# A hybrid encoder trunk: another order of the block steps, the norm and the table load where its stages meet

## The chip, the cores and the metric

The kernel runs on one core of a Trainium2 chip. The metric is the device time of one execution in microseconds. TensorE does the matrix products, VectorE (DVE), ScalarE (ACT) and GpSimd (POOL) the rest, and SyncE issues the loads of the weights.

## The reference

512 tokens and 16 learned meta tokens (528 in all) of width 1024, float32, pass two layers, each of three residual sub-layers behind an RMS norm:

```
for i in range(DEPTH):                                   # 2
    h = h + 0.5 * swiglu(rmsnorm(h, ffn1_norm[i]), ffn1_w_in[i], ffn1_w_out[i])
    hn = rmsnorm(h, mix_norm[i])
    h = h + (diff_attention(hn, ...) if i % 2 == 0 else gla_mixer(hn, ...))
    h = h + 0.5 * swiglu(rmsnorm(h, ffn2_norm[i]), ffn2_w_in[i], ffn2_w_out[i])
return rmsnorm(h, final_norm)[:, N_META:]
```

swiglu(h) is (silu(h @ w_g) * (h @ w_u)) @ w_out with an inner width of 2816. The attention is a differential one over 8 heads, block-causal; GLA is gated linear attention over 4 heads in chunks of 64.

## The kernel before, in words

**Stages.** The program is written out as a fixed order of instructions, and each engine runs its own in that order. The stages are a (SwiGLU), attention ("da"), b, c (SwiGLU of the next layer), GLA, and d. The residual stream lies in SBUF with features on partitions, as eight blocks `xr[0..7]` of 128 features by 528 tokens.

**Products.** A float32 operand is split into a high part (rounded, made by ScalarE) and a low part (the difference, made by VectorE); a product is three matrix products, high by high, high by low and low by high. Weights are split the same way as they come.

**A SwiGLU stage** (`ffn`, L679). The inner width is 22 blocks. A plain block takes four units S1, S3, S2, S4 of 24 matrix products. The others take seven units P1 to P7 of 12 products each, by a scheme with sums of quarters of the operands (`in_units`, L560). S1 and S3 read even blocks of the stream, S2 and S4 odd ones. The class `in_stream` (L568) lists the weight tasks: "cut" (ScalarE L637 makes the high part, VectorE L662 the low part) and "add" (VectorE L651, sums of weight quarters, four per block of seven). Split weights lie in a ring of nine slots. `to(n)` (L673) cuts the first n; in the stage, after each unit, tasks are issued until the weights lead by `AHEAD` = 6 units (L916 to L920). The second product of the stage (`out_piece`, L844, matrix products L857) works in six slabs of inner blocks; the last slab is the tail (L939 to L956).

**The norm** is not applied to the input but to the result of the first product, as a scale per token. `add_square` (L334) squares a finished block on ScalarE (L340) and adds it up on POOL (L344). `rms_scale` (L377) loads a function table into ScalarE (L370), sums over partitions by two matrix products with ones (L384), and makes the scale R by logarithm, exponential and a Newton step (L349 to L356). It is called behind unit S3 of block 0, in stage a behind S4 of block 1 (L929). A unit's result is scaled as it leaves PSUM (L734); where R does not exist yet it is copied (L736) and scaled later (L717). The units of plain blocks use four PSUM banks, so P1, the first unit of the next block, needs the bank of S1 and S2 to be empty.

**The end of a stage.** When block j of the output is done, VectorE adds it to the stream (L873 in a SwiGLU stage, L541 behind attention and GLA). Then `follow` (L502) starts the block's way into the next stage, a generator `next_block` (L462). For kind "seven" (into b, c, d) its steps are: on ScalarE the plain split's high part (L420), the square, and the scaled form (L434); on VectorE the low part (L425, two halves of an even block, one piece of an odd one) together with sums of quarters (L444 for an even block, L446 to L448 for an odd one); for an odd block then ScalarE's high part of the sums (L454); and VectorE's low part (L456). For kind "parts" (into attention and GLA) they are ScalarE's L468 and square, and VectorE's L471. `follow` first takes one step of every pending generator (`go_on`), then the new block's first step, then one more step of the old ones. So the steps of block j-1 come behind the addition of block j. `drain` takes what is left.

Behind attention and GLA, `finish_all` (L294) ends blocks 0 to 2 and collects what follows; blocks 3 to 7 run one after another (L1461), and at the start of each, `take` (L237) may split a chunk of the projection's weights two blocks ahead (ScalarE L223, VectorE L226). `ahead` is the next stage's weight stream: it is started behind block 5 and cut to 2, to 4 behind block 6 and to 5 at the end. In b's tail the same stands in `nxt.to(j - 2)` behind block j from 3 on. Output pairs of PSUM banks alternate between two places, so a block's products wait for the addition of the block before last.

Of the kernel before, what the change touches and what calls it, by code (L numbers as in the profile page):

```python
# [104 lines left out]
def hybrid_trunk_kernel(  # L105
# [271 lines left out]
    def rms_scale(acc, name, c0=0):  # L377
        hn = (L - c0) // 2
        table(LN_EXP)
# [82 lines left out]
    def next_block(kind, gcol, acc, j, c0, z=None):  # L462
# [11 lines left out]
        elif kind == "seven":  # L474
# [6 lines left out]
            rest()  # L481
            sums(i, tok, z[i], k)
# [11 lines left out]

    def go_on():
        for x in list(pending):
            try:
                next(x)
            except StopIteration:
                pending.remove(x)  # L500

    def follow(gen=None):  # L502

        go_on()
        before = list(pending)
        if gen is not None:
            next(gen, None)
            pending.append(gen)
        for x in before:
            try:  # L510
                next(x)
            except StopIteration:
                pending.remove(x)
# [19 lines left out]
    def project_out(nk, rhs, coef, gnext, name, tokens_only, c_next, apart=None):  # L533
# [4 lines left out]
        def out_block(j):  # L538
            def done(ps):
                for pv, xv in evacuation(ps, xr[j], tokens_only, j == apart):  # L540
                    dve.scalar_tensor_tensor(xv, pv, coef, xv, op0=ALU.mult, op1=ALU.add)  # L541
                rest = lambda: follow(next_block("seven", gnext, acc, j, c_next, z))
                if patient[0]:
                    later.append(rest)
# [134 lines left out]
    def ffn(stream, gain, acc, name, gnext, kind, nxt, aside=(), head=None, tok=False, behind=None):  # L679
# [8 lines left out]
        with tc.tile_pool(name=f"h_{name}", bufs=1) as hp:  # L688
# [22 lines left out]
            late = []  # L711
            bare = []
# [157 lines left out]
            def out_done(s, j):  # L870
                ps = outs.pop((s, j))
                for pv, xv in evacuation(ps, xr[j], tok):
# [29 lines left out]
            for i, u in enumerate(work):  # L902
# [4 lines left out]
                else:  # L907
                    product(*u)
                if behind and i <= KD:
# [9 lines left out]
                for _ in range(-(-(goal - stream.done) // between)):  # L919
                    stream.step()  # L920
# [3 lines left out]
                if len(u) == 3:  # L924
                    if u[2] == pieces(u[0]) - 1:
                        out_done(*u[:2])
                else:
                    evacuate(*u)
                    if u == ((1, "S4") if head else (0, "S3")):  # L929
                        R.append(rms_scale(acc, name, c0))  # L930
                        scale_bare()
                    if aside and u[1] in ("P4", "S4"):
# [6 lines left out]
            for j in range(KD):  # L939
# [7 lines left out]
                if j == 1 and kind == "parts":  # L947
# [3 lines left out]
                    load_to(2)  # L951
                out_done(tail, j)
                if kind == "parts" and j in (5, 6):
                    split_to(j - 5)
                if kind == "seven" and j >= 3:
                    nxt.to(j - 2)  # L956
# [95 lines left out]
    def diff_attention(acc, gnext, ahead):  # L1052
# [6 lines left out]
        with ExitStack() as es:  # L1059
# [401 lines left out]
            for j, b in enumerate(blocks[3:], 3):  # L1461
                run(b)
                if j == 5:
                    ahead.start()
                    ahead.to(2)
                if j == 6:
                    ahead.to(4)
            drain()
            ahead.to(5)
# [34 lines left out]
    def gla(acc, gnext, ahead):  # L1504
# [5 lines left out]
        with ExitStack() as es:  # L1510
# [346 lines left out]
            for j, b in enumerate(blocks[3:], 3):  # L1857
                run(b)
                if j == 5:
                    ahead.start()  # L1860
                    ahead.to(2)
# [161 lines left out]
```

## Time and profile before

| what | value |
|---|---|
| runs shown | 2094.09, 2098.22, 2100.36 us; median 2098.22 |
| the profiled execution | 2095.57 us |
| its span, first to last instruction | 2093.8 us |
| mean granted TensorE clock | 0.981 |
| matrix products | 14672 |
| VectorE, ScalarE, POOL instructions | 3095, 2046, 193 |

In rows of a timeline the first two numbers are the start and the length in microseconds from the start of the span, and the bracket at the end is the idle time of the engine ahead of the row with what ended it; xN is the number of instructions merged into the row. A row of the waits names who waited for whom, then the total, the times and the longest.

### The profile page before, as it was taken

Reading aid. Unit: us, or ns where it says so; the run is one execution under the profiler, and the core shown is the slowest. Engines: PE = TensorE matmul, PEld = TensorE weight load, DVE = VectorE, ACT = ScalarE, POOL = GpSimd, SP = SyncE. Lnnn points to the kernel's source line nnn. Section 1 sums busy time; section 2 is a strip of 40 time slices with the busy share of each in tenths; the row PEclk is TensorE's granted clock in tenths of the full one; section 3 lists DMA queues with packets and bytes.
Section 4 is the critical chain, followed back from the end, with each engine's and each line's share of the span. In section 5 each row is a group of like instructions: output and inputs, shape, how many; then the busy total and the mean of one; then the engine's idle time right before and its main releaser. Section 6 shows DMA issues by size and latency. Waiting matters only on the chain.

```text
span 2093.8 us, 36697 instructions
## 1 busy us (share of the span) xinstructions
PE 1984.3 (95%) x14672; PEld 1875.5 (90%) x14672; DVE 1681.0 (80%) x3095; ACT 1023.1 (49%) x2046; POOL 263.6 (13%) x193
## 2 busy tenths in 40 slices
PE   7899999999899989999997999999899989999997
PEld 7899999877787979999997999999788878999995
DVE  7888887688888789888878988887666678988884
ACT  6444444455555554444445444444654555544443
POOL 2000000534332200000001000000633210000002
PEclk9999999999999999999999999999999999999998
DMA  4233323111111223333322333332122222333331
GB/s 146 88 103 107 96 97 107 51 51 41 41 42 40 71 81 109 99 101 99 104 77 67 111 101 97 98 102 85 55 78 73 64 91 82 116 100 98 106 101 41
DMA packets 66285, 178.73 MB, mean 85 GB/s; under 512 B 7345, under 2 KB 13618, under 8 KB 66114
## 3 DMA queue, kind: packets, MB, share of 16 engines
q1 hardware_dynamic: 65792, 176.25, 27.1%
q8 instruction: 115, 1.88, 0.4%
q14 instruction: 56, 0.46, 0.1%
q10 hardware_dynamic: 322, 0.13, 0.0%
HBM read 174.26 MB, written 2.10 MB: 84 GB/s over the span
## 4 chain that ended last, share of the span: by engine, by line
PE 72%; DVE 18%; ACT 6%; issue 3%; POOL 0%; DMA 0%; SPq 0%; DVEq 0%; ACTq 0%; POOLq 0%
PE ps_ao L857 6%; PE ps_co L857 6%; PE ps_bA L806 6%; PE ps_bo L857 5%; PE ps_cA L806 5%; PE ps_aA L806 5%; PE ps_do L857 5%; PE ps_dA L806 4%; PE ps_bD L806 3%; PE ps_cD L806 3%; PE ps_aD L806 3%; PE ps_dak L270 2%; PE ps_dD L806 2%; DVE ra L662 2%; PE ps_bB L806 1%
## 5 line engine op out<-in xcount | busy, mean ns | idle before, releaser
L637 ACT CAST ra<-fa 128x512 fp32r<-128x512 f32 x630 | 376.2, 618 | 166.7 <-DVE fa L651 165.9
L662 DVE TENSOR_TENSOR ra<-fa,ra 128x512 fp32r<-128x512 f32 x630 | 425.5, 685 | 22.2 <-ACT ra L637 16.4
L651 DVE TENSOR_TENSOR fa<-fa 128x512 f32<-128x512 f32 x328 | 219.7, 686 | 2.8
L834 DVE TENSOR_TENSOR ra<-fa,ra 128x512 fp32r<-128x512 f32 (+1 forms) x160 | 101.4, 636 | 68.0 <-ACT ra L833 66.7
L226 POOL TENSOR_TENSOR ra<-fa,ra 128x1024 fp32r<-128x1024 f32 x51 | 123.7, 2427 | 154.2 <-ACT ra L223 130.3
L806 PE MATMUL ps_bA<-ra 128*128 128x264 f32 x1008 | 134.7, 286 | 5.0 <-DVE ftb L734 4.0
L806 PE MATMUL ps_cA<-ra 128*128 128x264 f32 x1008 | 134.1, 285 | 4.8 <-DVE ftc L734 3.6
L806 PE MATMUL ps_dA<-ra 128*128 128x256 f32 x1008 | 132.1, 283 | 5.0 <-DVE ftd L734 3.1
L806 PEld LDWEIGHTS ps_dA<-ra 128*128 128x128 f32 x1008 | 127.8, 190 | 9.5 <-issue 3.3
L806 PEld LDWEIGHTS ps_bA<-ra 128*128 128x128 f32 x1008 | 127.8, 190 | 5.9 <-issue 4.2
L806 PEld LDWEIGHTS ps_cA<-ra 128*128 128x128 f32 x1008 | 127.2, 189 | 5.7 <-issue 3.7
L806 PE MATMUL ps_aA<-ra 128*128 128x264 f32 x912 | 122.1, 286 | 7.3 <-DVE fta L734 6.9
L806 PEld LDWEIGHTS ps_aA<-ra 128*128 128x128 f32 x912 | 115.8, 190 | 8.0 <-issue 7.1
L833 ACT CAST ra<-fa 128x512 fp32r<-128x512 f32 (+1 forms) x160 | 91.6, 575 | 0.0
L857 PE MATMUL ps_bo<-ra 128*128 128x264 f32 x624 | 86.0, 284 | 2.7 <-DVE xr L873 1.8
L857 PE MATMUL ps_co<-ra 128*128 128x264 f32 x624 | 85.8, 284 | 0.8 <-ACT ra L833 0.7
L857 PE MATMUL ps_ao<-ra 128*128 128x264 f32 x624 | 85.7, 283 | 0.9 <-DVE ra L834 0.9
L857 PE MATMUL ps_do<-ra 128*128 128x512 f32 x309 | 82.1, 395 | 0.9 <-ACT ra L833 0.7
L857 PEld LDWEIGHTS ps_bo<-ra 128*128 128x128 f32 x624 | 79.7, 188 | 3.5 <-issue 2.2
L857 PEld LDWEIGHTS ps_co<-ra 128*128 128x128 f32 x624 | 79.7, 188 | 1.3 <-ACT ra L833 0.9
L857 PEld LDWEIGHTS ps_ao<-ra 128*128 128x128 f32 x624 | 79.7, 188 | 1.1 <-DVE ra L834 1.1
L223 ACT CAST ra<-fa 128x1024 fp32r<-128x1024 f32 x64 | 66.8, 1046 | 4.3 <-issue 1.8
(529 smaller groups left out, 4341.7 us busy)
## 6 DMA issues: line engine op xcount, KB each, us to landing
fa<-in_f_in SPq DMA_DIRECT2D x174, 512.0 KB, 3.6
fa<-in_f_out SPq DMA_DIRECT2D x160, 256.0 KB, 2.7
fa<-in_da_in SPq DMA_DIRECT2D x24, 512.0 KB, 3.6
fa<-in_gla_in SPq DMA_DIRECT2D x24, 512.0 KB, 3.6
fa<-in_f_out SPq DMA_DIRECT2D x32, 128.0 KB, 2.1
fa<-in_da_out SPq DMA_DIRECT2D x8, 512.0 KB, 3.6
fa<-in_gla_out SPq DMA_DIRECT2D x8, 512.0 KB, 3.4
xr<-in_xT SPq DMA_DIRECT2D x8, 264.0 KB, 5.4
```

The lines of the kernel that those rows point to most:

```text
L223: act.copy(h, w)
L226: eng.tensor_tensor(out=l, in0=w, in1=h.bitcast(F32), op=ALU.subtract)
L270: nc.tensor.matmul(put(b, at, at + c1 - c0), w[:, ws], x[:, c0:c1], start=first, stop=last,)
L637: act.copy(self.parts(n)[0], self.source(i))
L651: dve.tensor_tensor(out=self.raw(f, x), in0=self.raw(f, a), in1=self.raw(f, b), op=ALU.add)
L662: dve.tensor_tensor(out=l, in0=self.source(i), in1=h.bitcast(F32), op=ALU.subtract)
L806: nc.tensor.matmul(banks[k, f], w[:, ws], v, start=(p in ("P1", "P2", "P7") and i == 0 and c == 0), stop=(i == NQ - 1 and c == 2), skip_gr ...
L833: act.copy(h, raw)
L834: dve.tensor_tensor(out=l, in0=raw, in1=h.bitcast(F32), op=ALU.subtract)
L857: nc.tensor.matmul(ps[:, b, : a1 - a0], w[:, ws], x[:, a0:a1], start=(f == f0 and i == 0), stop=(f == f1 - 1 and i == 2),)
```

## The change

It makes these edits. (1) In `next_block`, kind "seven", the low part and the sums become two steps. (2) `go_on` takes one step of the newest pending generator, one of each older one, then two more of the newest; it is called ahead of the addition of a block (behind it for blocks 0 to 2 of attention and GLA), and `follow` only takes the new block's first step. (3) The table load leaves `rms_scale`; it is issued behind block 3 of the tails of a, b and c, and in stage a ahead of its norm. (4) The norm is asked for behind unit S1 of block 0, in stage a behind S1 of block 2; a unit's evacuation while there is no R is issued behind the next unit's products. (5) In the first 16 items of a stage at most three weight tasks follow one item. (6) In b's tail `nxt.to(j - 2)` moves ahead of the addition of block j; behind attention and GLA the next stream is cut to 2 behind block 6 and to 3 at the end. (7) Stage a has four plain blocks instead of three and starts its ring two slots on; the two asides (lambda terms, gate weights) follow P4 units only.

```diff
     def rms_scale(acc, name, c0=0):
         hn = (L - c0) // 2
-        table(LN_EXP)
...
             yield
             rest()
+            yield
             sums(i, tok, z[i], k)
...
+    def steps_of(gen, n=1):
+        for _ in range(n):
+            try:
+                next(gen)
+            except StopIteration:
+                pending.remove(gen)
+                return
+
     def go_on():
-        for x in list(pending):
-            try:
-                next(x)
-            except StopIteration:
-                pending.remove(x)
-
-    def follow(gen=None):
-
-        go_on()
-        before = list(pending)
-        if gen is not None:
-            next(gen, None)
-            pending.append(gen)
+        if not pending:
+            return
+        *before, last = pending
+        steps_of(last)
         for x in before:
-            try:
-                next(x)
-            except StopIteration:
-                pending.remove(x)
+            steps_of(x)
+        if last in pending:
+            steps_of(last, 2)
+
+    def follow(gen):
+        next(gen, None)
+        pending.append(gen)
...
             def done(ps):
+                if not patient[0]:
+                    go_on()
...
                 if patient[0]:
-                    later.append(rest)
+                    later.append(lambda: (go_on(), rest()))
...
             def out_done(s, j):
                 ps = outs.pop((s, j))
+                if s == len(slabs) - 1:
+                    go_on()
...
                     product(*u)
+                    if waiting:
+                        evacuate(*waiting.pop())
+                    if u == ((2, "S1") if head else (0, "S1")):
+                        if head:
+                            table(LN_EXP)
+                        R.append(rms_scale(acc, name, c0))
+                        scale_bare()
...
-                for _ in range(-(-(goal - stream.done) // between)):
+                n_ = -(-(goal - stream.done) // between)
+                for _ in range(min(n_, 3) if i < 2 * KD else n_):
                     stream.step()
...
+                elif not R:
+                    waiting.append(u)
                 else:
                     evacuate(*u)
-                    if u == ((1, "S4") if head else (0, "S3")):
-                        R.append(rms_scale(acc, name, c0))
-                        scale_bare()
-                    if aside and u[1] in ("P4", "S4"):
+                    if aside and u[1] == "P4":
                         aside.pop(0)()
...
+                if kind == "seven" and j >= 3:
+                    nxt.to(j - 2)
                 out_done(tail, j)
+                if kind and j == 3:
+                    table(LN_EXP)
                 if kind == "parts" and j in (5, 6):
                     split_to(j - 5)
-                if kind == "seven" and j >= 3:
-                    nxt.to(j - 2)
...
                 if j == 5:
                     ahead.start()
+                if j == 6:
                     ahead.to(2)
-                if j == 6:
-                    ahead.to(4)
             drain()
-            ahead.to(5)
+            ahead.to(3)
...
-        "a": in_stream(f1_in[0], f1_out[0], 0, 3),
+        "a": in_stream(f1_in[0], f1_out[0], 2, 4),
```

## Rows read from the trace of the kernel before

**Rows 1.** The page's table of engines: busy us (share of the span) xinstructions.
```profile
PE 1984.3 (95%) x14672; PEld 1875.5 (90%) x14672; DVE 1681.0 (80%) x3095; ACT 1023.1 (49%) x2046; POOL 263.6 (13%) x193
```
**Rows 2.** The waits of TensorE over the whole span.
```profile
PE ps_dS L792 <- DVE ra L425: 4.5, 1, 4.5
...
PE ps_ss_gla L384 <- POOL acc_c L344: 3.1, 1, 3.1
```
**Rows 3.** The timeline of TensorE at the entries into a, b and c.
```profile
42.31 11.94 PE L792 MATMUL ps_aS<-ra 128*128 128x264 f32 x96
61.13 2.98 PE L806 MATMUL ps_aA<-ra 128*128 128x264 f32 x12 [6.88 <-DVE fta L734]
...
738.63 6.37 PE L792 MATMUL ps_bS<-ra 128*128 128x264 f32 x38 [4.52 <-DVE ra L425]
...
755.71 2.98 PE L806 MATMUL ps_bA<-ra 128*128 128x264 f32 x12 [3.97 <-DVE ftb L734]
...
1113.25 6.77 PE L792 MATMUL ps_cS<-ra 128*128 128x264 f32 x38 [5.57 <-DVE ra L425]
...
1130.33 2.36 PE L806 MATMUL ps_cA<-ra 128*128 128x264 f32 x12 [3.56 <-DVE ftc L734]
```
**Rows 4.** The timeline of VectorE from b's tail into c.
```profile
1088.56 0.71 DVE L873 SCALAR_TENSOR_TENSOR xr<-ps_bo,xr 128x528 f32<-128x528 f32 x1 [1.04 <-PE ps_bo L857]
...
1096.42 0.70 DVE L873 SCALAR_TENSOR_TENSOR xr<-ps_bo,xr 128x528 f32<-128x528 f32 x1
...
1098.40 0.42 DVE L448 SCALAR_TENSOR_TENSOR ftb<-ftb 128x264 f32<-128x264 f32 x1
1100.75 0.69 DVE L662 TENSOR_TENSOR ra<-fa,ra 128x512 fp32r<-128x512 f32 x1 [1.93 <-ACT ra L637]
1101.36 0.70 DVE L873 SCALAR_TENSOR_TENSOR xr<-ps_bo,xr 128x528 f32<-128x528 f32 x1
1101.97 1.25 DVE L456 TENSOR_TENSOR ra<-ftb,ra 128x1056 fp32r<-128x1056 f32 x1
1103.14 1.99 DVE L425 SCALAR_TENSOR_TENSOR ra<-xr,vec,ra 128x264 fp32r<-128x264 f32 x2
...
1110.93 0.70 DVE L873 SCALAR_TENSOR_TENSOR xr<-ps_bo,xr 128x528 f32<-128x528 f32 x1
...
1120.25 2.02 DVE L651 TENSOR_TENSOR fa<-fa 128x512 f32<-128x512 f32 x3
...
1125.27 0.43 DVE L350 TENSOR_SCALAR nA_c<-ps_ss_c 128x264 f32<-128x264 f32 x1 [0.96 <-ACT R_c L349]
...
1129.16 0.69 DVE L662 TENSOR_TENSOR ra<-fa,ra 128x512 fp32r<-128x512 f32 x1
```
**Rows 5.** The timeline of ScalarE behind attention (first row) and in b's tail.
```profile
716.73 1.04 ACT L223 CAST ra<-fa 128x1024 fp32r<-128x1024 f32 x1
...
1097.15 0.93 ACT L420 ACTIVATE ra<-xr,vec 128x264 fp32r<-128x264 f32 x2 [2.46 <-DVE xr L873]
...
1099.14 1.06 ACT L454 CAST ra<-ftb 128x1056 fp32r<-128x1056 f32 x1
1100.10 0.61 ACT L637 CAST ra<-fa 128x512 fp32r<-128x512 f32 x1
1102.09 0.74 ACT L420 ACTIVATE ra<-xr,vec 128x528 fp32r<-128x528 f32 x1 [1.38 <-DVE xr L873]
...
1103.90 0.60 ACT L637 CAST ra<-fa 128x512 fp32r<-128x512 f32 x1
...
1123.46 1.28 ACT L370 ACT_TABLE_LOAD   x1
```
**Rows 6.** The timeline of VectorE behind attention: additions 3 and 7, a chunk's split.
```profile
713.84 0.69 DVE L541 SCALAR_TENSOR_TENSOR xr<-ps_dao,xr 128x528 f32<-128x528 f32 x1
...
718.47 1.21 DVE L226 TENSOR_TENSOR ra<-fa,ra 128x1024 fp32r<-128x1024 f32 x1
...
736.31 0.70 DVE L541 SCALAR_TENSOR_TENSOR xr<-ps_dao,xr 128x528 f32<-128x528 f32 x1
```
**Rows 7.** The timeline of POOL: the last addition of squares in b's tail.
```profile
1113.07 1.31 POOL L344 TENSOR_TENSOR acc_b<-acc_b,sq 128x528 f32<-128x528 f32 x1 [3.45 <-ACT sq L340]
```

More of the change, by code (lines that the diff above doesn't have):

```diff
@@ L711, in ffn @@
             late = []
+            waiting = []
             bare = []
@@ L1860, in gla @@
                     ahead.start()
+                if j == 6:
                     ahead.to(2)
-                if j == 6:
-                    ahead.to(4)
             drain()
-            ahead.to(5)
+            ahead.to(3)
             return nacc
     ins = {
-        "a": in_stream(f1_in[0], f1_out[0], 0, 3),
+        "a": in_stream(f1_in[0], f1_out[0], 2, 4),
         "b": in_stream(f2_in[0], f2_out[0], 0, 1),
```

## Prediction

> **What bounds the kernel now.** I read the busy table first: TensorE is busy 95% of the span and no other engine over 80% [rows 1]. So the time is the products plus TensorE's waits, and a change of order can only move the waits. The list of waits on TensorE comes next: apart from the attention's scores, its long ones stand where stages meet [rows 2]. The timeline of TensorE there [rows 3] shows the pattern of an entry into a SwiGLU stage b, c or d. The first product S1 of the new stage breaks off until VectorE has split the stream's block 6 (L425: 4.52 us in b, 5.57 in c, 4.5 in d [rows 2, 3]), and four products later the first product P1 waits for a PSUM bank, which VectorE frees only after the norm (L734: 3.97 and 3.56). Stage a waits 6.88 us for L734 too. Who is late is VectorE, so the question is what its queue, and ScalarE's which feeds it, look like in the new order; both run in the order of the program, as the rows of the tails show [rows 4, 5].
>
> **Blocks at the end of b (entry into c).** Now an addition (L873) goes first, ScalarE then makes the block's plain, square and scaled forms, and VectorE meanwhile splits and sums the block before. Additions 2 and 7 stand at 1088.56 and 1110.93: 22.4 us for five [rows 4]. The new order puts between two additions, on VectorE: one weight of the next stage (L662, which waits for ScalarE's L637), then the split and the sums of the block just added, the cut (L456) of the odd block before it, and only then the next addition. L637 stands on ScalarE behind the three forms of that same block. So each step waits for the one before it, across both engines, and VectorE has nothing to do while ScalarE works. That is the weight placement as before seen from the queue: ahead of addition j instead of behind j-1 is the same place, and what was ahead of it on VectorE is now behind it.
> Durations, start to start. After an even block ScalarE runs cut, forms and L637: 1097.15 to 1100.71, 3.56 us; after an odd one, with no cut ahead, 1102.09 to 1104.50, 2.41 us, plus 0.73 from the addition's start to ScalarE's [rows 4, 5]. Then VectorE: L662 0.6; split and three sums of an odd block 1.78 (1096.42 to 1098.82 less the addition's 0.62), of an even block, two splits and one sum, 1.3 (estimate from the same row; 1.99 for the splits alone is what they take beside POOL's addition); L456 1.17 behind an even block. An even step is 3.6 + 0.6 + 1.3 + 1.2 = 6.7, an odd one 3.2 + 0.6 + 1.8 = 5.6. From addition 2 to 7: three even steps, two odd ones, and the table load of 1.28 that now stands on ScalarE behind block 3 [rows 5]: 20.1 + 11.2 + 1.3 = 32.6 us, where it is 22.4. Addition 2 itself comes about 2.7 late: two steps without a weight are 0.7 + 1.8 + 1.1 = 3.6 each against the products' 24 x 0.124 = 3.0 [rows 3], and the first starts behind block 0's forms. Addition 7 lands at about 1123.9, **13.0 late**; bounds 9 (each step 0.8 shorter) and 16 (the splits caught by POOL each time).
> The Trainium skill, ScalarE: Activation LUTs, What ACT_TABLE_LOAD costs, gives 1283 ns for the load and some 1380 ns of drain at every switch. The row shows the load alone, 1.28 us; by the page the move would cost this chain 1.4 more. No run here shows the drain, and the sum does without it.
>
> **From addition 7 to P1.** Now 1130.33 - 1110.93 = 19.4 us in c, and 755.71 - 736.31 = 19.4 in b [rows 3, 4, 6]. New, in c: form and square 0.7 + 0.65 + 0.6, POOL's addition 1.31 [rows 7], which holds VectorE's sums too (they fall on it, as L425 does now at 1.99), sums 1.05, cut 1.06 and its low part 1.2: 6.65. The norm's sum comes in beside this, since S1 alone stands ahead of it. Then the norm on VectorE, 1125.27 to 1129.16: 3.9. Behind it come the weights that stood ahead of it: the stream may take three tasks a product now, and the first bank is freed after the third product, so four L662 (0.6) and four L651 (2.02 for three) go first: 5.1; and 0.6 to P1. Together 16.2, **3.2 less**: the norm comes early, and most of that is given back by the weights behind it. In b and d only three weights are cut in advance instead of five, so it is one L662 ahead and one more behind: 17.4, **2.0 less**. Bound of both: no gain, and 5 where the weights fit into the norm's waits.
> c: 13.0 - 3.2 = +9.8.
>
> **Ends of attention and GLA (entries into b and d).** A block here has 48 products, 5.9 us [rows 3], so there is more room, but three things take it. (1) In block 2 the step (L425, sums, L454) goes ahead of ScalarE's forms: L454 of block 1 (1.06) now precedes block 2's forms, which wait for those sums. Addition 3, now at 713.84, then stands behind split, cut and sums of block 2: forms from about 713.8, split 0.5 after, 0.8, 1.2, 0.4: about 717. (2) In blocks 4 and 5 the split of a projection chunk (L223 1.04 on ScalarE, then L226 1.21 on VectorE) stands between the addition and the block's split; now its wait for ScalarE is covered by the splits of the block before [rows 5, 6]. Additions 3 to 4: 0.7 + 1.8 + 1.0 + 1.2 + 1.8 = 6.5; 4 to 5: cut 1.0 + 2.1 + 1.0 + 1.2 + 1.3 + 1.2 less overlaps = 7.5. (3) 5 to 6 is 4.0 (no chunk left); 6 to 7 has two weights: 1.0 + 2.1 + 0.6 + 1.2 + 1.3 + 1.2 = 7.2. Addition 7 lands at 717 + 25.2 = 742.2 instead of 736.31, **6.0 late**; less 2.0: b +4.0. Bounds -4 (the additions keep up with the products) and +6.5. Products wait too, for block 3's and 5's PSUM pair, but under the same chain. d repeats b with shorter rows: +4.0.
>
> **Stage a.** The fourth plain block costs 96 products in place of 84: 12 x 0.124 = +1.5 [rows 3]. The norm is asked for 24 products later (3.0), of which 2.3 come back, as neither the table load (1.28) nor a cast of 1.06 stands between its sum and the logarithm. Behind it four weight tasks leave the queue ahead of L734 (three L651 2.02 and one L662, 2.7 in all), and one L651 more: 3.3. So the 6.88 wait shortens by about 2.6: net -1.1, and -0.4 for weight work saved later: **-1.5**. The lambda terms go behind P4, where the function table is that of Silu: two more loads, 2.6 us of ScalarE, with VectorE waiting behind them. Cover is the lead of six products; bounds -4 and +2.
>
> **Entries into the mixers.** VectorE's low part of block 6 no longer follows addition 7, so it meets POOL's last addition less. The wait for POOL is 3.1 us in GLA [rows 2]: -1.0 there, -0.3 in attention; bounds 0 and -3.1. The removed table loads stood beside VectorE's weights or TensorE's sums, so nothing more is gained. The wait list that holds evacuations in stage a changes no place in VectorE's queue: 0.
>
> **Sum.** 9.8 + 4.0 + 4.0 - 1.5 - 1.3 = +15.0. The profiled execution took 2095.57 us (span 2093.8); 2110.6. The median of the runs shown, 2098.22, is 2.65 above it; I give 2111. A shorter or longer wait ahead of P1 also moves TensorE's clock: 12 products behind such a wait take 2.98 us in b where 96 took 11.94 [rows 3]; 1.5 per entry either way, in the range only.
>
> **Rivals.** (A) The forecast, +15: two engines in a chain where they ran beside each other; its own range 2102 to 2120.
> (B) Faster. The products pace the additions, and the steps fall into VectorE's waits for them, as the words of the change say. Place: additions 3 to 7 of attention and GLA. If these take no more than the 22.5 us of now [rows 6] with addition 3 on time, S1 no longer waits: -4.5, -4.5, -5.6 and, with -1.5, -1.3 and 3 of the waits before P1, about -20: 2078. For it: VectorE has idle stretches such as the 1.93 ahead of L662 [rows 4]. Against: these are waits for ScalarE, which the new order lengthens.
> (C) Balance. c loses 9.8 as above, but b and d keep up and gain 4 each; with a and the mixers -1: 2097.
> Weight of each: A hangs on the program's order alone and on durations that each have a row, 0.68; B 0.20; C 0.12. A measurement of this kernel tells about 0.3% (6.3 us) from no change. Slower 0.68, same 0.12, faster 0.20. The range 2086 to 2121 takes in C, the milder part of B and the upper bounds of A; the rest of B is left out.
>
> **What would show it.** Right: in b's tail L662 idles some 2.5 us for L637 at each block from 3 on, additions stand 5.5 to 6.7 us apart, and S1 of c resumes near 1122 on the old scale; additions 3 to 7 of attention take 25 us; in b and c five or more weight tasks stand between the norm's last step and L734. Wrong: additions within 5 us of each other in b's tail, or addition 7 of attention on TensorE's heels, with S1 unbroken.

## The result and the profile after

The changed kernel takes 2117.62 us (median of 4 runs, 2114.54 to 2119.60) against 2099.29 for the kernel before beside it: a ratio of 1.009, 95% interval 1.0075 to 1.0105, so slower by 0.9%. The profiled execution took 2114.54 us with a span of 2112.8, that is 19.0 us more than the span before, at nearly the same granted clock (0.979 against 0.981). The two traces can therefore be set against each other place by place.

The page's table of engines of the changed kernel, to be read against [rows 1]:

```profile
PE 1994.7 (94%) x14684; PEld 1881.7 (89%) x14684; DVE 1669.1 (79%) x3086; ACT 1020.4 (48%) x2040; POOL 262.3 (12%) x193
```

VectorE, ScalarE and POOL all do a little less than before, yet the span is longer. That is the picture of waits, not of work. The list of TensorE's waits, to be read against [rows 2]:

```profile
PE ps_bo L864 <- DVE xr L882: 9.7, 4, 3.9
...
PE ps_glao L270 <- DVE xr L547: 5.0, 3, 2.5
PE ps_aS L799 <- DVE fta L741: 4.3, 1, 4.3
PE ps_dao L270 <- DVE xr L547: 4.2, 2, 3.1
...
PE ps_bA L813 <- DVE ftb L741: 2.5, 1, 2.5
```

The 4.5 us of S1 in b and d are gone from the list, as are the 3.97 ahead of P1 of b. In their place stand waits of the output products for the additions themselves (L882 in b's tail, L547 behind the mixers): TensorE now stops one step earlier, for a PSUM pair that is not yet added.

The timeline of VectorE in b's tail and behind the norm of c, to be read against [rows 4]:

```profile
1094.64 0.69 DVE L882 SCALAR_TENSOR_TENSOR xr<-ps_bo,xr 128x528 f32<-128x528 f32 x1
1098.36 0.85 DVE L668 TENSOR_TENSOR ra<-fa,ra 128x512 fp32r<-128x512 f32 x1 [3.02 <-ACT ra L643]
...
1106.17 0.69 DVE L668 TENSOR_TENSOR ra<-fa,ra 128x512 fp32r<-128x512 f32 x1 [3.90 <-ACT ra L643]
...
1127.95 0.70 DVE L882 SCALAR_TENSOR_TENSOR xr<-ps_bo,xr 128x528 f32<-128x528 f32 x1
...
1138.56 0.69 DVE L668 TENSOR_TENSOR ra<-fa,ra 128x512 fp32r<-128x512 f32 x1
1139.16 2.02 DVE L657 TENSOR_TENSOR fa<-fa 128x512 f32<-128x512 f32 x3
...
1143.68 0.77 DVE L741 TENSOR_TENSOR ftc<-ps_cS,R_c 128x264 f32<-128x264 f32 x2
```

Additions 2 and 7 stand 33.31 us apart (22.37 before). At every block from 3 on VectorE idles 2.5 to 3.9 us for the high part of the weight, L643. The longest one holds the table load; ScalarE's timeline shows it directly ahead of that high part:

```profile
1104.22 1.28 ACT L370 ACT_TABLE_LOAD   x1
1105.51 0.62 ACT L643 CAST ra<-fa 128x512 fp32r<-128x512 f32 x1
```

Behind attention the same pattern stands with the projection's chunk (L226) in the weight's place; VectorE, to be read against [rows 6]:

```profile
714.30 0.70 DVE L547 SCALAR_TENSOR_TENSOR xr<-ps_dao,xr 128x528 f32<-128x528 f32 x1
717.90 1.23 DVE L226 TENSOR_TENSOR ra<-fa,ra 128x1024 fp32r<-128x1024 f32 x1 [2.90 <-ACT ra L223]
...
724.90 1.23 DVE L226 TENSOR_TENSOR ra<-fa,ra 128x1024 fp32r<-128x1024 f32 x1 [3.45 <-ACT ra L223]
...
740.39 0.70 DVE L547 SCALAR_TENSOR_TENSOR xr<-ps_dao,xr 128x528 f32<-128x528 f32 x1
```

TensorE at the entries into b and c, to be read against [rows 3]:

```profile
737.48 4.45 PE L799 MATMUL ps_bS<-ra 128*128 128x264 f32 x22 [0.35 <-DVE ra L668]
743.89 1.16 PE L383 MATMUL ps_ss_b<-acc_da,ones 128*128 128x264 f32 x4 [1.96 <-POOL acc_da L344]
...
757.90 2.11 PE L813 MATMUL ps_bA<-ra 128*128 128x264 f32 x12 [2.55 <-DVE ftb L741]
...
1126.04 3.45 PE L799 MATMUL ps_cS<-ra 128*128 128x264 f32 x14 [2.94 <-DVE ra L424]
...
1144.16 1.74 PE L813 MATMUL ps_cA<-ra 128*128 128x264 f32 x12 [1.38 <-DVE ftc L741]
```

The 19.0 us come together as follows. Each line is the shift of one place of the trace against the same place before, less the shift of the place ahead of it. The places are the starts of the instructions named, and additions are counted from 0, as the blocks are.

| place, from what to what | forecast | measured |
|---|---|---|
| stage a, to the first attention product (387.47, now 385.17) | -1.5 | -2.3 |
| entry into attention, to its first projection (397.26, now 394.51) | -0.3 | -0.45 |
| attention, to addition 0 behind it (702.00, now 698.50) | 0 | -0.75 |
| entry into b, to P1 (755.71, now 757.90) | +4.0 | +5.7 |
| b, to addition 0 of its tail (1084.22, now 1087.07) | 0 | +0.7 |
| entry into c, to P1 (1130.33, now 1144.16) | +9.8 | +11.0 |
| c and the entry into GLA, to its first projection (1487.44, now 1500.24) | -1.0 | -1.0 |
| GLA, to addition 0 behind it (1682.94, now 1696.85) | 0 | +1.1 |
| entry into d, to P1 (1735.98, now 1755.49) | +4.0 | +5.6 |
| d, to the end of the span | 0 | -0.5 |
| sum | +15.0 | +19.0 |

### The profile page after: what moved, and what is told of

It reads as the page before. It is cut to its first block, busy times and chain, and to the rows that moved or that the text cites. A ratio compares the mean times of both kernels' runs of the same rounds, so it can differ in the third digit from the quotient of the medians.

```text
span 2112.8 us, 36705 instructions
## 1 busy us (share of the span) xinstructions
PE 1994.7 (94%) x14684; PEld 1881.7 (89%) x14684; DVE 1669.1 (79%) x3086; ACT 1020.4 (48%) x2040; POOL 262.3 (12%) x193
## 4 chain that ended last, share of the span: by engine, by line
PE 70%; DVE 20%; ACT 6%; issue 3%; POOL 0%; DMA 0%; SPq 0%; DVEq 0%; ACTq 0%; POOLq 0%
PE ps_co L864 6%; PE ps_ao L864 6%; PE ps_bo L864 5%; PE ps_bA L813 5%; PE ps_cA L813 5%; PE ps_do L864 5%; PE ps_aA L813 5%; PE ps_dA L813 4%; PE ps_bD L813 3%; DVE ra L668 3%; PE ps_cD L813 3%; PE ps_aD L813 2%; PE ps_dak L270 2%; PE ps_dD L813 2%; DVE fa L657 1%
## 5 line engine op out<-in xcount | busy, mean ns | idle before, releaser
L643 ACT CAST ra<-fa 128x512 fp32r<-128x512 f32 x627 | 374.5, 618 | 170.6 <-DVE fa L657 169.6
L668 DVE TENSOR_TENSOR ra<-fa,ra 128x512 fp32r<-128x512 f32 x627 | 424.7, 687 | 35.8 <-ACT ra L643 30.1
L657 DVE TENSOR_TENSOR fa<-fa 128x512 f32<-128x512 f32 x324 | 217.0, 687 | 2.8
L226 POOL TENSOR_TENSOR ra<-fa,ra 128x1024 fp32r<-128x1024 f32 x51 | 122.7, 2406 | 154.9 <-ACT ra L223 125.8
L813 PE MATMUL ps_aA<-ra 128*128 128x264 f32 x864 | 114.6, 284 | 0.2 <-ACT fta L761 0.2
L813 PEld LDWEIGHTS ps_aA<-ra 128*128 128x128 f32 x864 | 108.8, 188 | 0.8 <-ACT fta L761 0.4
L799 PE MATMUL ps_aS<-ra 128*128 128x264 f32 x384 | 55.3, 310 | 16.7 <-DVE fta L743 6.0
```

Of the source, the lines that this page charges most:

```text
L226: eng.tensor_tensor(out=l, in0=w, in1=h.bitcast(F32), op=ALU.subtract)
L643: act.copy(self.parts(n)[0], self.source(i))
L657: dve.tensor_tensor(out=self.raw(f, x), in0=self.raw(f, a), in1=self.raw(f, b), op=ALU.add)
L668: dve.tensor_tensor(out=l, in0=self.source(i), in1=h.bitcast(F32), op=ALU.subtract)
L799: nc.tensor.matmul(banks["S", f, p, k], w[:, ws], v, start=(p in ("S1", "S3") and i == 0 and c == 0), stop=(p in ("S2", "S4") and i == NQ ...
L813: nc.tensor.matmul(banks[k, f], w[:, ws], v, start=(p in ("P1", "P2", "P7") and i == 0 and c == 0), stop=(i == NQ - 1 and c == 2), skip_gr ...
```

## The experiments

The theory is the forecast's: the new step order puts VectorE and ScalarE into one chain where they ran beside each other. The main rival is that another part of the change costs: the early norm with the weights behind it, or the table load in the tail. In each run that was timed the kernel before ran beside it; its median lay between 2096.97 and 2097.57 us, and the ratios are to it. A ratio is therefore the better measure where two runs below are compared; the changed kernel has 1.0090.

**e1: the step order undone, all else of the change kept.**

```diff
             rest()
-            yield
             sums(i, tok, z[i], k)
...
             def out_done(s, j):
                 ps = outs.pop((s, j))
-                if s == len(slabs) - 1:
-                    go_on()
...
-                if kind == "seven" and j >= 3:
-                    nxt.to(j - 2)
                 out_done(tail, j)
...
+                if kind == "seven" and j >= 3:
+                    nxt.to(j - 2)
             drain()
```

(`go_on` and `follow` are again those of the kernel before, here and behind attention and GLA; that part of the edit is left out.)

> The changed kernel with the step order alone undone: the steps of a finished block follow the next addition again, and b's weight follows it too. Norm behind S1, at most three weight tasks an item, two and three weights cut ahead, table load in the tail and the fourth plain block stay. Theory (the step order puts VectorE and ScalarE in one chain): additions 3 to 7 of attention again take about 22.5 us and additions 2 to 7 of b about 22.4 (26.1 and 33.3 in the changed kernel); S1 of b, c and d breaks off again for the split of block 6; what stays is stage a's 2.3 and up to 2 us an entry from the norm, so 2090 to 2098 us. Rival (the early norm with its weights behind it, or the table load in the tail, is what costs): still 2108 or more, with first products P1 of b, c and d as late as in the changed kernel.

Measured: 2095.41 us median of 12 runs, ratio 0.9994 (0.9982 to 1.0005): about 1% under the changed kernel and no different from the kernel before. Additions 3 to 7 of attention take 21.26 us, additions 2 to 7 of b 22.7, and S1 of c breaks off for 5.57 us for the split of block 6, as it did before. The rival falls: the norm, its weights and the table load in the tail cost nothing that can be seen. But they bring little too, as VectorE at the entry into c shows. TensorE's row of that break comes first, then VectorE:

```profile
1116.81 3.45 PE L792 MATMUL ps_cS<-ra 128*128 128x264 f32 x14 [5.57 <-DVE ra L424]
```

```profile
1114.48 0.70 DVE L873 SCALAR_TENSOR_TENSOR xr<-ps_bo,xr 128x528 f32<-128x528 f32 x1
...
1126.74 0.43 DVE L356 SCALAR_TENSOR_TENSOR R_c<-nT_c,R_c 128x264 f32<-128x264 f32 x1
1127.09 0.68 DVE L661 TENSOR_TENSOR ra<-fa,ra 128x512 fp32r<-128x512 f32 x1
1127.69 2.01 DVE L650 TENSOR_TENSOR fa<-fa 128x512 f32<-128x512 f32 x3
...
1132.20 0.77 DVE L734 TENSOR_TENSOR ftc<-ps_cS,R_c 128x264 f32<-128x264 f32 x2
```

The norm ends 12.6 us after addition 7 (1127.09 less 1114.48) where it ended 18.2 after it before (1129.16 less 1110.93 [rows 4]), but 5.1 us of weight tasks (the stretch from 1127.09 to 1132.20) now stand between it and the evacuation; P1 follows addition 7 by 18.3 us instead of 19.4.

**e2: the step order alone, put on the kernel before** (the edits (1), (2) and the first half of (6) of the change).

> The kernel before with the step order alone: steps ahead of the next addition, low part and sums as two steps, b's weight ahead of the addition; norm, table load, weights cut ahead and stage a as before. Theory: the whole loss is here, 2112 to 2126 us; addition 7 comes about 7 us late behind attention and GLA and about 12.5 late in b (13.8 in the changed kernel less the table load). Rival (the order is harmless and the norm or the weights cost): 2103 us or less.

Measured: 2119.96 us, ratio 1.0111 (1.0094 to 1.0128). Additions 0 to 7 take 39.62 us in b's tail where they took 26.71, so addition 7 is 12.9 late; behind attention and GLA it is 9.4 and 9.3 late, more than the 7 expected, as four weights instead of two stand behind blocks 5 and 6 there. P1 follows addition 7 of b by 17.4 us, with the norm still behind S3. The additions of b's tail, 0, 2 and 7:

```profile
1090.69 0.71 DVE L882 SCALAR_TENSOR_TENSOR xr<-ps_bo,xr 128x528 f32<-128x528 f32 x1 [2.12 <-PE ps_bo L864]
...
1098.27 0.69 DVE L882 SCALAR_TENSOR_TENSOR xr<-ps_bo,xr 128x528 f32<-128x528 f32 x1
...
1130.31 0.70 DVE L882 SCALAR_TENSOR_TENSOR xr<-ps_bo,xr 128x528 f32<-128x528 f32 x1
```

The whole loss is in this one part; together with e1 this settles the question between theory and rival.

**e3: the weight of b's tail moved within the changed kernel.**

```diff
                 if s == len(slabs) - 1:
                     go_on()
+                    if kind == "seven" and j >= 3:
+                        nxt.to(j - 2)
...
-                if kind == "seven" and j >= 3:
-                    nxt.to(j - 2)
                 out_done(tail, j)
```

> The changed kernel with one edit: in b's tail the weight of the next stage is cut between the steps of block j-1 and the addition of block j, no longer ahead of those steps. Theory (chain of both engines, the weight's two halves in its middle): VectorE no longer idles for the weight's high part ahead of a split; the sums still wait for ScalarE's scaled form. Additions 2 to 7 of b take 25 to 29 us instead of 33.3, addition 7 and P1 of c come 4 to 8 us earlier, and the time is 2110 to 2114 us. Rival 1 (the weight only fills VectorE's idle time beside ScalarE): within 1 us of the changed kernel. Rival 2 (the weight was the whole loss of this tail): additions 2 to 7 in 22.4 us, 11 us less.

Measured: 2114.23 us, ratio 1.0075 (1.0062 to 1.0088), an interval that still overlaps with the changed kernel's; it is the trace that shows the gain. Additions 2 to 7 of b take 29.8 us, and P1 of c comes 3.6 earlier from the first output product of b on. Rival 1 falls, rival 2 too, and the theory's 25 to 29 was too hopeful. VectorE, and then POOL, show what took part of it back:

```profile
1107.59 0.69 DVE L668 TENSOR_TENSOR ra<-fa,ra 128x512 fp32r<-128x512 f32 x1 [1.66 <-ACT ra L643]
...
1111.66 1.35 DVE L443 TENSOR_TENSOR ftb<-ftb 128x264 f32<-128x264 f32 x1
```

```profile
1110.54 2.19 POOL L344 TENSOR_TENSOR acc_b<-acc_b,sq 128x528 f32<-128x528 f32 x1 [5.58 <-ACT sq L340]
```

The weight's high part still stands on ScalarE behind the cut of the sums (L453), which waits for VectorE's sums, so VectorE idles 1.66 us for it. And the sum L443, 0.43 us in the changed kernel, now falls on POOL's addition and takes 1.35, in each of the three even steps. Moving the weight out of the middle of the chain gives back 3.5 us, a third of the tail's loss of 10.9. The rest stays without it: the chain itself, with the table load and the sums beside POOL in it. The two steps of the changed kernel that hold no weight at all say the same: 3.21 and 4.36 us from addition 0 to 1 and 1 to 2, where there were 1.44 and 2.90.

**e4: stage a's part alone, put on the kernel before** (edits (4), (5) and (7) for stage a only).

> The kernel before with the edits of stage a alone: four plain blocks, ring two slots on, norm behind S1 of block 2, held evacuations, at most three weight tasks an item in a, asides behind P4. All other stages as before. Theory (the gain of a is a gain by itself): the end of a comes 2.3 us earlier in the trace, the wait ahead of P1 is about 4.3 us instead of 6.88, and everything behind it moves by that; time 2.3 us under the kernel before, less than a run can tell. Rival: a's weights are only put off, so the end of a moves by less than 0.5.

Measured: 2093.13 us, one run. The end of a comes at 383.8 instead of 387.47, 3.7 earlier, and the wait behind the norm is 4.3 us. The gain of a is one by itself. Its size is less sure than one trace says: in the ten traces with these edits, that of the changed kernel among them, the first attention product starts between 383.8 and 385.6, in the three without between 387.1 and 387.5. So the gain is somewhere between 1.5 and 3.7 us. The scatter lies ahead of the norm: from the first product of its sum, at 43.5 to 45.3, to the first attention product nine of the ten traces take 340.3 to 340.4 us, and that of e3 340.9.

**e5 and e6: fewer weights behind the norm**, in e5 on the kernel of e1, in e6 on the changed kernel.

```diff
-                for _ in range(min(n_, 3) if i < 2 * KD else n_):
+                cap = 1 if not head and i < 4 else 3
+                for _ in range(min(n_, cap) if i < 2 * KD else n_):
```

> The kernel with the old step order and the early norm (run e1), and at most one weight task behind each of the first four units of b, c and d instead of three. Theory (VectorE's work between the norm and the first scaled result is what gave the early norm's gain back): three tasks instead of nine stand between the norm's last step and the evacuation, P1 follows the last S4 product almost at once, 2 to 2.7 us earlier at each of the three entries, and the time is 2088 to 2091 us, or 5 to 7 under run e1. Rival (a debt that is collected later): TensorE waits for weights some units on, and the time stays within 2 us of run e1.

> The changed kernel with one edit: at most one weight task behind each of the first four units of b, c and d instead of three. Theory: the waits of P1 for the evacuation (2.5, 1.4 and 2.6 us) go, since six tasks fewer stand behind the norm; the additions stay as late as in the changed kernel, so 2111 to 2114 us. Rival (the products S3, S2, S4 run at half clock behind their wait and P1 could not come earlier anyway): 2116 to 2119.

Measured: e5 2094.23 us, ratio 0.9990 (0.9981 to 0.9999), 1.2 under e1, whose runs overlap with it; e6 2120.47 us, ratio 1.0119 (1.0105 to 1.0133), at any rate not under the changed kernel. P1 does come earlier: counted from addition 7 ahead of it, 2.8, 2.0 and 2.8 us in b, c and d of e5 and 2.8, 3.0 and 2.8 in e6. But from P1 to the first output product of the stage TensorE's waits add up to 4.9, 4.4 and 5.3 us in e5, where they were 3.2, 2.1 and 3.4 in e1, and in e6 to 4.9, 5.1 and 5.1, where the changed kernel has 1.7, 2.1 and 1.8. TensorE in b of e5 shows the debt:

```profile
750.91 1.61 PE L806 MATMUL ps_bA<-ra 128*128 128x264 f32 x12
...
755.14 1.73 PE L806 MATMUL ps_bA<-ra 128*128 128x264 f32 x12 [1.15 <-ACT ftb L747]
...
763.73 1.73 PE L806 MATMUL ps_bA<-ra 128*128 128x264 f32 x12 [1.99 <-ACT ftb L754]
```

P1 follows without a wait, and the weights that were put off then stand in front of the next evacuations. So the rival of e5 is right for most of it, and my theory of e6 is wrong: the weights behind the norm are put off or done early, not saved. The rival of e6 falls too, since P1 could come earlier.

**e7: the table load back into the norm of c.**

```diff
-                        if head:
+                        if head or name == "c":
                             table(LN_EXP)
...
-                if kind and j == 3:
+                if kind == "parts" and j == 3:
                     table(LN_EXP)
```

> The changed kernel with the function table of the norm into c loaded in the norm again, not behind block 3 of b's tail. Theory (the load stands in the chain of both engines): additions 2 to 7 of b take 1.3 us less, 32.0 instead of 33.3; at the norm of c the load stands beside the sum over partitions and costs little, so P1 of c comes about 1 us earlier; the time falls by less than a run can tell. By the Trainium skill, ScalarE: Activation LUTs, What ACT_TABLE_LOAD costs, a switch also drains some 1380 ns, and additions 2 to 7 would take 2.7 less. Rival (the load hides behind VectorE's work): no change of the additions.

Measured: 2114.8 us, one run, no difference that it can show. In the trace additions 2 to 7 of b take 32.07 us instead of 33.31, 1.24 less, and P1 of c follows addition 0 by 56.5 instead of 57.1. VectorE, then ScalarE at the norm:

```profile
1095.01 0.69 DVE L882 SCALAR_TENSOR_TENSOR xr<-ps_bo,xr 128x528 f32<-128x528 f32 x1
...
1127.08 0.70 DVE L882 SCALAR_TENSOR_TENSOR xr<-ps_bo,xr 128x528 f32<-128x528 f32 x1
```

```profile
1132.62 1.28 ACT L370 ACT_TABLE_LOAD   x1
1133.92 0.48 ACT L349 ACTIVATE R_c<-ps_ss_c,epst 128x264 f32<-128x264 f32 x1
```

The load costs its own 1.28 us where it stands in the chain, and half of that at the norm.

**e8, e9 and e11: the weight's high part ahead of the addition.** If the price of a weight in a tail is VectorE's idle time for its high part, then that part should be issued while ScalarE waits for the addition, and only the low part behind it. e8 does this on e5, e11 on e1, e9 on the kernel before.

```diff
+                if kind == "seven" and j >= 3:
+                    nxt.hi(nxt.done)
                 out_done(tail, j)
...
             for j, b in enumerate(blocks[3:], 3):
+                if j == 6:
+                    ahead.hi(0)
+                    ahead.hi(1)
                 run(b)
```

(in e9 the weights 2 and 3 there)

> As e5, and ScalarE's high part of the next stage's weight is issued ahead of the addition (in b's tail from block 3 on, behind attention and GLA for two weights ahead of block 6), while VectorE's low part stays behind it. Theory (a weight costs a tail what VectorE idles for its high part, because the high part stands on ScalarE behind the forms of the block just added): the 1.9 us ahead of each low part in b's tail go, steps of 4.6 to 5 us become 3 to 4, addition 7 of b comes 4 to 9 us earlier, attention and GLA gain up to 1.9 each; 2077 to 2085 us. Rival (another wait takes its place: the sums fall on POOL's addition, or the cut of the sums waits for ScalarE): additions 4.5 us apart as before and 2087 or more.

> The kernel before with one edit: ScalarE's high part of a weight of the next stage is issued ahead of the addition instead of behind the forms of its block (b's tail from block 3 on; behind attention and GLA two weights ahead of block 6). Nothing else of the change. Theory (what a weight costs at these places is VectorE's idle time for its high part): in b's tail two of the five steps from addition 2 to 7 fall from 4.9 to 2.9 us as in run e8, addition 7 of b comes 3.5 to 4.5 us earlier, addition 7 of attention and GLA 1 to 2 earlier, and the time is 2088 to 2093 us. Rival (run e8 owed its gain to the early norm, with which this went together): P1 of c comes less than 1.5 us earlier, 2095 or more.

> As run e8, but with up to three weight tasks behind each unit again (that is, run e1 with the high parts ahead). Theory (the weights are put off, not saved): P1 of b, c and d comes 1.5 to 3 us later than in run e8, the stage behind each takes that much less, and the time is that of run e8 within 2 us. Rival (one task behind a unit is the better rule by itself): 3 us or more slower than run e8.

Measured: e8 2089.68 us, ratio 0.9967 (0.9952 to 0.9981); e11 2089.07 us, ratio 0.9953 (0.9941 to 0.9965). Both beat the kernel before by 0.3 to 0.5%, and the changed kernel by 1.2 to 1.4%. In b's tail additions 2 to 7 take 19.0 us in both (22.7 in e1); behind attention the step from 6 to 7 falls from 5.5 to 3.5, behind GLA to 4.4 in e8 and 3.5 in e11. ScalarE and VectorE in e8:

```profile
1093.04 0.62 ACT L636 CAST ra<-fa 128x512 fp32r<-128x512 f32 x1
1093.56 0.73 ACT L419 ACTIVATE ra<-xr,vec 128x528 fp32r<-128x528 f32 x1
```

```profile
1092.28 0.69 DVE L873 SCALAR_TENSOR_TENSOR xr<-ps_bo,xr 128x528 f32<-128x528 f32 x1
...
1094.60 2.00 DVE L424 SCALAR_TENSOR_TENSOR ra<-xr,vec,ra 128x264 fp32r<-128x264 f32 x2
...
1096.86 0.68 DVE L661 TENSOR_TENSOR ra<-fa,ra 128x512 fp32r<-128x512 f32 x1
1097.47 0.69 DVE L873 SCALAR_TENSOR_TENSOR xr<-ps_bo,xr 128x528 f32<-128x528 f32 x1
```

The low part L661 has no idle time ahead of it any more. I had expected 1.9 us to go at each of them; in e1 and in the kernel before such a wait stood at every other one only (1.93 and 1.92 us, [rows 4] show one). Every other step, as the one to 1092.28, is down to 2.9 us, the pace of the products; the steps between stay at 5.0 to 5.2: VectorE has hardly any idle time left in them, and the splits of an even block take 2.00 us beside POOL's addition. That part of the rival is right, and it is why the gain was 4.6 us over e5 and 6.3 over e1 where I expected 9 or more. e11 equals e8: P1 follows addition 7 by 2.4 to 3.2 us more in b, c and d of e11, and the stretch from P1 to the first output product is 2.2 to 4.6 us shorter there. One weight or three behind a unit makes no difference, as e5 and e6 had said.

In e9 one part of the computation is another: behind attention and GLA the two high parts are put into slots that still hold the weights of block 6, so block 6 there is made from other weights, and its products wait for them:

```profile
728.04 13.50 PE L270 MATMUL ps_dao<-ra 128*128 128x264 f32 x96 [8.44 <-ACT ra L637]
```

That is 8.4 and 8.0 us in the two mixers, and the time, 2109.48 us with a ratio of 1.0060 (1.0046 to 1.0074), says nothing on b and d. Its b tail can be read: additions 0 to 7 take 23.30 us instead of 26.71, and P1 of c comes 3.0 us earlier from the first output product of b on, with the old norm. So this gain is not owed to the early norm. The same edit behind the mixers of the kernel before, with free slots, was not tried.

**e10: the projection's chunk moved within the changed kernel**, from the start of a block to between the steps and the addition.

```diff
-        soon(lambda n=i + reach[0]: split_to(n))
+        if hold[0] is None:
+            soon(lambda n=i + reach[0]: split_to(n))
+        else:
+            hold[0].append(i + reach[0])
...
                 if not patient[0]:
                     go_on()
+                while hold[0]:
+                    split_to(hold[0].pop(0))
```

(`hold[0]` is a list while blocks 3 to 7 run, and None otherwise.)

> The changed kernel with one edit: behind attention and GLA the split of a projection's chunk stands between the steps of the block before and the addition, no longer between an addition and the steps of its block. Theory (my third point on b's and d's entries: the chunk's two halves stand in the chain of both engines there): steps 3 to 4 and 4 to 5, 6.45 and 7.75 us in the changed kernel, become about 1 shorter each, P1 of b and d comes 1 to 3 earlier, 2112 to 2116 us. Rival (the chunk only fills the time in which VectorE waits for ScalarE's forms): the steps stay, or grow, since the chunk's own cut then stands on VectorE ahead of the addition; 2117 or more.

Measured: 2118.87 us, ratio 1.0099 (1.0084 to 1.0113), not under the changed kernel. The steps 3 to 4 and 4 to 5 behind attention are 7.69 and 5.89 us where they were 6.45 and 7.75: 0.6 less for both, not 2. VectorE:

```profile
723.80 1.22 DVE L227 TENSOR_TENSOR ra<-fa,ra 128x1024 fp32r<-128x1024 f32 x1 [2.09 <-ACT ra L224]
724.94 0.70 DVE L553 SCALAR_TENSOR_TENSOR xr<-ps_dao,xr 128x528 f32<-128x528 f32 x1
```

The chunk now waits behind ScalarE's cut of the sums, which waits for the sums: another crossing between the two engines in place of the one removed. And one sum in each of the two steps now falls on POOL's addition and takes 1.11 and 1.37 us, where both took 0.43. The rival's outcome came true, by these two costs, and the time of 2117 or more with it. What the chunk's old place cost by itself is not shown, as the new costs stand against it.

## Why the prediction was right, step by step

The forecast was 2111 us in a range of 2086 to 2121; 2117.62 lies in it, on the side and by the mechanism of rival (A). Rival (B) falls with the number it named: additions 3 to 7 of attention take 26.1 us, not 22.5 or less. Rival (C) falls with the entries into b and d, which lost 5.7 and 5.6 us where they were to gain 4 each. The signs named for being right came, if not to the microsecond: VectorE waits for the weight at each block from 3 on, additions stand 5.65 to 6.93 us apart, S1 of c resumes at 1126.04, which is 1123.2 on the old scale (the 2.85 us by which addition 0 came later taken off), and nine weight tasks in b and eight in c stand behind the norm.

**b's tail.** Right in mechanism, and close in size. L668 waits for L643 at each block from 3 on, as forecast with 2.5 us; it is 2.5 to 3.9. Even steps, those behind an even block, were forecast with 6.7 us and take 6.92 (6.89 the last), the odd one without a load 5.6 and takes 5.65, the one with the load 6.9 and takes 6.92. From addition 2 to 7 that is 33.3 for 32.6. Addition 2 was to come 2.7 late and came 3.2 late: the step of the odd block 1 takes 4.36, not 3.6, as its first sum falls on POOL's addition. e2 and e1 show that all of this is the step order, but for the table load (e7).

**From addition 7 to P1.** Forecast 16.2 in c and 17.4 in b; measured 16.21 and 17.51. The order of the tasks behind the norm is the one counted: four L668 and four L657 in c, five L668 and four L657 in b, ahead of L741. "Most of that is given back by the weights behind it" is what e1 shows in its purest form (5.1 us of tasks behind a norm that ended 5.6 sooner), and e5 and e6 add what the prediction had not said: putting these tasks off doesn't keep the gain either. But the 3.2 and 2.0 us are not the early norm's alone, as the prediction had it. With the old norm and the new step order, in e2, P1 follows addition 7 by 17.35 us in c and 18.07 in b: 2.0 and 1.3 us of the gain come with the step order, which splits block 6 ahead of addition 7. The early norm and its weights add 1.1 and 0.6, and in e1 they bring 1.1 and 0.5 by themselves (18.29 and 18.89 us). So about a third of the gain that the prediction gives to the early norm is its own.

**Ends of attention and GLA.** The term was mis-sized, 4.0 for 5.7 and 5.6. Addition 3 was to stand at 717 on the old scale and stood at 717.8 (714.30 plus the 3.5 by which all came earlier); the four steps behind it were forecast at 6.5, 7.5, 4.0 and 7.2 and take 6.45, 7.75, 4.38 and 7.51. Both halves fall short by 0.8 to 0.9. The sums that I took at their own length stand beside POOL's addition in part of the blocks: the sum ahead of addition 3 takes 1.34 us instead of 0.42, which is the whole first half, and the first sum of the step from 5 to 6 takes 1.11. The rest of the second half is arithmetic. The terms given for the step from 6 to 7 add up to 7.4 and not to 7.2, and the overlaps of 0.3 taken off the step from 4 to 5 did not come. My second point, that the chunk between addition and split makes the steps long, is left open by e10: moved out of that place the two steps gain 0.6 us, with new costs in them.

**Stage a.** The wait behind the norm shortened by 2.6 us as forecast (6.88 to 4.29, now at a unit of the fourth plain block). The gain is 2.3 instead of 1.5, and 3.7 in e4. The waits for the copies out of PSUM that precede the norm (L736, now L743) fall by 0.8, from 6.8 to 6.0 us, but they stand in the part of the stage that scatters by 1.8 us from trace to trace, so 1.5 and 2.3 cannot be told apart here. The list of waits has none for the lambda terms.

**Mixer entries.** The wait for POOL in GLA falls from 3.05 to 2.59, half of the 1.0 forecast. That the row of c and GLA reads -1.0 as forecast is luck: the other half stands in c, where the stretch from P1 to the first output product takes 24.87 us at a granted clock of 1.00 and took 25.45 at 0.93 before. The prediction had the clock behind P1 in its range only, and put it down to the wait ahead of P1. The wait's length does not settle it: behind 2.11 us of it in e1 the stretch has 1.00 granted, behind 1.86 in e7 0.93. Attention and GLA themselves shifted by -0.75 and +1.1, which the change doesn't touch. Between all the traces the same two stretches differ by up to 6.6 and 5.2 us, and they go with the granted clock: attention takes 304.7 us at 0.96 before, 304.0 at 0.97 in the changed kernel and 309.7 at 0.94 in e1; GLA 195.5 at 1.00, 196.6 at 0.99 and 200.4 at 0.97. So these shifts are no effect of the change; the last section shows such a place.

**The table load.** By the Trainium skill, ScalarE: Activation LUTs, What ACT_TABLE_LOAD costs, a switch takes the load and some 1380 ns of drain. The trace differs: the high part L643 starts 0.01 us behind the load's end in the changed kernel, the norm's logarithm 0.02 behind it in e7, where the load itself started 0.02 behind the cast ahead of it, and e7's tail is shorter by 1.24 us, the load alone. The sum did right to leave the drain out.

## What to carry to other kernels

Where two engines pass a block back and forth, ask of each instruction moved whether it stands ahead of or behind work that waits for the other engine: steps of block j ahead of the addition of j + 1 look like less delay, but turn two queues that ran side by side into one chain, here 22.4 us into 32.0 (e2, the step order alone). Filler work with a part on each engine belongs where the first part's engine waits anyway: the high part of a weight ahead of the addition instead of behind its block's forms gained 4.6 and 6.3 us for eight lines (e8 and e11), where the reordering of all steps lost some 20. Work put behind a critical step instead of ahead of it is a gain only if the stage behind has room for it; look a few units on before counting it.

## What the runs showed of the hardware

Which VectorE operation meets POOL's addition decides up to 1.1 us of each step. A sum of 0.43 us takes 1.07 to 1.56 beside it, two splits of 0.89 take 2.00, and POOL's own 1.31 become 2.19 when VectorE's operation started first. In e3 the sum L443, started at 1111.66, ends at 1113.01, just behind POOL's addition (1110.54 and 2.19: 1112.73): it does not share, it waits. The Trainium skill, SBUF — State Buffer, Who interferes with whom, says that a VectorE instruction with two SBUF inputs contends with a GpSimd instruction that reads SBUF, and that the port pair they share is an exclusive lock; this trace agrees.

One profiled execution can hold several microseconds of TensorE's clock that belong to no edit. That of e1 took 2101.4 us, 6 above the median of its 12 runs. The view of busy times by stretch shows one such place, the start of GLA, with the granted clock in the column behind POOL's:

```profile
1489.00:1552.00 63.00, 59.00 (x370) 52.64 (x371) 39.25 (x60) 34.23 (x63) 26.91 (x13) 0.91 0.24 67
```

In the kernel before the stretch from 1487 to 1550 has 1.00 granted. The same 48 projection products behind the norm of GLA, in e1 and then in the kernel before:

```profile
1489.35 8.03 PE L270 MATMUL ps_gva<-ra 128*128 128x264 f32 x48 [1.14 <-DVE nA_gla L350]
```

```profile
1487.44 6.10 PE L270 MATMUL ps_gva<-ra 128*128 128x264 f32 x48 [1.54 <-DVE nA_gla L350]
```

They took 8.03 us at a granted clock of 0.73, so part of them at 1.2 GHz, and 6.10 at 1.00, that is 2.4 GHz, though both came behind the same two waits, for POOL and for the norm. So a difference of one stage that the edit does not touch was not read as an effect of the edit in any run above.
